# State carried between chunks of 128 tokens in place of scores across chunks, in a hybrid GLA and mLSTM block

## The chip, the cores and the metric

The kernel runs on one core of a Trainium2 chip. The metric is the device time of one execution in microseconds (us), and the figure given is the median over runs. The profiled execution is one more run, of which every instruction is recorded.

## The reference, cut to what matters

One layer of a block with two kinds of recurrent heads, four each: gated linear attention (GLA) and mLSTM. Both run over 512 latent tokens in both directions, starting from a state that 256 context tokens leave. Per head the key width is 128 and the value width 256. All is float32.

```python
# GLA, one direction:  S_t = diag(a_t) S_{t-1} + k_t v_t^T ;  o_t = S_t^T q_t
bcum = jnp.cumsum(ac, axis=2)                      # log decays within a chunk
k_to_end = kc * jnp.exp(b_end[:, :, None, :] - bcum)
s_new = jnp.exp(b_end)[..., None] * s + jnp.einsum('bhik,bhiv->bhkv', k_to_end, vc)
o = (jnp.einsum('bhji,bhiv->bhjv', scores, vc)     # scores within the chunk, with decays
     + jnp.einsum('bhjk,bhkv->bhjv', qc * jnp.exp(bcum), s))
# mLSTM, one direction: one forget gate and one input gate per token and head, running maximum m
c_new = carry_scale[..., None, None] * c + jnp.einsum('bhi,bhik,bhiv->bhkv', w, kc, vc)
n_new = carry_scale[..., None] * n + jnp.einsum('bhi,bhik->bhk', w, kc)
s = jnp.einsum('bhjk,bhik->bhji', qc, kc) * jnp.exp(d_log - m_q[..., None])   # masked
h = num / jnp.maximum(jnp.abs(den), jnp.exp(-m_q))[..., None]
```

The result does not depend on the chunk length: one may compute scores over any stretch of tokens and carry a state for the rest. Around this stand adaLN modulation, one input projection for all heads, a per-head norm with output gates, an output projection, and a gated feed-forward part with a 3x3 depthwise convolution.

## The kernel before, in words

The kernel runs in stages: modulation and the first projection (0 to 186 us), the heads (186 to 822), the output gates (to 965) and the output projection (to 1090), then the feed-forward part. Large products are done in three matmuls of float32r parts (`mm3`): each weight block is loaded as `raw`, ACT casts it to `hi`, DVE subtracts to get `lo` (`load_split`). The products inside a head are plain float32, which the trace shows as two PE instructions each.

In the head stage PE's order is written out by hand (`pinned`, so every matmul keeps program order). `weave` mixes two generators: the stages of head h, and the projection of head h+1 (`project_steps`, six pieces per weight block, 1.04 to 1.44 us by its own estimate). Each `yield x` in a head's code asks for x us of projection work at that place, so that PE has something to do while DVE and ACT prepare the next product. What is left of the projection runs after the head. For heads 0 and 1 `first_stages` is used (both were projected together), for the others `stages`.

A head's float32 products go to PSUM through `psb`. Its pool `psB` has two banks; the other six (`psA`) hold the six projection results that are being accumulated. A bank is handed on when its last reader is done.

A GLA head (`gla`) works on four blocks of 128 tokens. `bt[d]` holds the running sum of log decays within each block, per direction d; `b2[d]` continues it over blocks. Scores within a block come in seven levels (distances 1, 2, 4 to 64): at each level the decays relative to a border are formed (`level_decays`: two DVE subtractions, two ACT exponentials), multiplied by q and k (DVE), multiplied on PE (`sl`, four products) and put into `scd` where a mask says so (DVE `copy_predicated`). Two more levels, 128 and 256, cover scores across blocks, using `b2` and its values at block ends (`ends`), and are copied to `sc1` and `sc2` by ACT. After level 1 the state of the context `s0` is formed (`cst`), and `qi`, q with its decay since the start. The output `po` of each block is the sum of six products: `qi` with `s0` for both directions, the block's own scores with v, and the scores of three other blocks with their v. While levels 2 to 6 run, the preparation of the next head (`gla_prep`) advances one step after each of them through `next(after, None)`: two decay products `dec` (one per direction, 512 tokens), two `cdec` (context), then `csum`. Each of the first four is followed by `log_sigmoid`, three ACT operations and one DVE operation (`la`, `cla`), which reads the bank again at its end.

An mLSTM head (`mlstm`) forms for both directions the exponentials `ed` of the gates for all pairs of blocks on the causal side (ACT), zeroes half of the diagonal blocks (POOL `affine_select`), multiplies them by the scores `s` (PE, four products of 512 columns; DVE), and sums into `po` one product with the context state `c0` and one per block on the causal side, for each block and direction. The value tile has two more columns of ones, which give the denominator. `ml_gates`, after the last GLA head, prepares per-token columns `acol`, `thr`, and `wc` for the context.

During mLSTM heads and later, `fill()` inserts pieces of the modulation (`mod_chunk`: two DVE operations on 512 columns; `mod_sums`, `mod_end`: small PE products through `psb`).

Of the kernel before, what the change touches and what calls it, by code (L numbers as in the profile page):

```python
# [11 lines left out]
F32 = mybir.dt.float32  # L12
# [6 lines left out]
P = 128  # L19
# [51 lines left out]
def block_kernel(ctx: ExitStack, tc: tile.TileContext, a: dict, out: bass.AP):  # L71
# [411 lines left out]
    gccol = states.tile([P, 2, H], F32, name="gccol")  # L483
    wc = states.tile([P, 2, CJ, H], F32, name="wc")
# [168 lines left out]
    def gla_prep(h, out):  # L653
# [36 lines left out]
        yield  # L690

        b2 = [ytile(10 + d, f"b2{h}{d}") for d in range(2)]
        for d in range(2):
            order = list(range(TJ)) if d == 0 else list(range(TJ - 1, -1, -1))
            j = order[0]
            V.tensor_copy(b2[d][:, P * j : P * j + P], bt[d][:, P * j : P * j + P])
            for p, j in zip(order, order[1:]):
                e = P * p + P - 1 if d == 0 else P * p
# [3 lines left out]
        ends = wtile(f"ends{h}", "ends", 2, 2, 3)  # L702
        for d in range(2):
            src = b2[d][:, P - 1 : 3 * P : P] if d == 0 else b2[d][:, P : 3 * P + 1 : P]
            for i, sgn in enumerate((-DECAY, DECAY)):
                V.tensor_scalar(out=ends[:, i, d, :], in0=src, scalar1=sgn, scalar2=None, op0=ALU.mult)
        out.update(bt=bt, b2=b2, kd=kd, ends=ends)
# [28 lines left out]
    def gla(h, pair, qk, v, kn, vn, yT, prep, fill, after, pending):  # L736
        bt, b2, kd, ends = (prep[n] for n in ("bt", "b2", "kd", "ends"))

        sc = wtile(f"sc{h}", "sc", 2, TJ, P)
        scd, sc1 = sc[:, 0], sc[:, 1]  # L740
        sc2 = [ytile(12 + i, f"sc2{h}{i}", (P, 2, 2 * P)) for i in range(2)]
        s0 = wtile(f"s0{h}", "state", 2, DV + 2)
        ps = psb(f"sd{h}", (P, TJ, P))
# [5 lines left out]
        for lv, b in enumerate(LEVELS + [P, 2 * P]):  # L749
            if b < P:  # L750
                ex = prep["ex"][lv] if lv < 2 else level_decays(h, lv, bt)
            else:
                ex = wk2.tile([P, 2, T], F32, name=f"ex{h}_{lv}", tag="ex")
                for i in range(T // (2 * b)):
                    e = 2 * i if b == P else 1
                    for s in range(2):
                        for d in range(2):

                            at = 2 * b * i + (b if s == d else 0)
                            S.activation(ex[:, s, at : at + b], b2[d][:, at : at + b], AF.Exp,  # L760
                                         scale=-DECAY if s else DECAY, bias=ends[:, s, d, e : e + 1])
# [5 lines left out]
            if b <= P:  # L767
                ps = psb(f"sl{h}_{lv}", (P, TJ, P))
                for i in range(TJ):
                    j = i if b < P else i ^ 1  # L770
                    mm(ps[:, i, :], ex[:, 1, P * i : P * i + P], ex[:, 0, P * j : P * j + P], start=True, stop=True)
                if b < P:
                    V.copy_predicated(scd, msk[:, lv, :].unsqueeze(1).to_broadcast([P, TJ, P]), ps)
                else:
                    S.copy(sc1, ps)
            else:
                for half in range(2):
                    ps = psb(f"sl{h}_{lv}_{half}", (P, 2, 2 * P))
                    for ii in range(2):
                        i = 2 * half + ii  # L780
                        j0 = 2 * P * (1 - half)
                        mm(ps[:, ii, :], ex[:, 1, P * i : P * i + P], ex[:, 0, j0 : j0 + 2 * P],
                           start=True, stop=True)
                    S.copy(sc2[half], ps)
            if lv == 0:
                pending()
            yield fill
            if lv in (2, 3, 4, 5, 6, 8):
                next(after, None)
            if lv == 1:  # L790

                for j in range(CJ):
                    mul(kd[:, :, j], kd[:, :, j], kn[j].unsqueeze(1).to_broadcast([P, 2, DK]))
                ps = psb(f"cst{h}", (P, 2, DV))
                for d in range(2):
                    for j in range(CJ):
                        mm(ps[:, d, :], kd[:, d, j, :], vn[j][:, 0:DV], start=(j == 0), stop=(j == CJ - 1))
                S.copy(s0[:, :, 0:DV], ps)
                qi = wtile(f"qi{h}", "qi", 2, T)
                for d in range(2):  # L800
                    S.activation(qi[:, d, :], b2[d], AF.Exp, scale=DECAY)
                mul(qi, qi, qk[0].unsqueeze(1).to_broadcast([P, 2, T]))
                yield 1
        ssq = wtile(f"ssq{h}", "ssq", TJ)
        junk = wtile(f"junk{h}", "kn", DV)
        ob = wtile(f"ob{h}", "tmp", TJ, DV)
        for j in range(TJ):
            po = psb(f"po{h}_{j}", (P, DV))
            js = slice(P * j, P * j + P)
            j2 = P * (j % 2)  # L810
# [11 lines left out]
    def ml_gates():  # L822
# [36 lines left out]
        dg = wk.tile([36, H], F32, name="dg", tag="st1")  # L859
        for d in range(2):  # L860
# [10 lines left out]
            end = TC - 1 if d == 0 else T  # L871
            V.tensor_scalar(out=negg[rows[d], :], in0=gmx[rows[d], lat0[d] : lat0[d] + T], scalar1=-1.0,
                            scalar2=None, op0=ALU.mult)
            V.tensor_scalar(out=dg[rows[d], :], in0=e, scalar1=gmx[rows[d], end : end + 1], scalar2=None, op0=ALU.mult)
            pg = psb(f"pgc{d}", (P, H))
            mm(pg, cst[rows[d], C_ONE : C_ONE + 1].to_broadcast([H, P]), dg[rows[d], :], start=True, stop=True)
            V.tensor_copy(gccol[:, d, :], pg)
            yield 1.4
        for d in range(2):
            for j in range(CJ):  # L880
                sub(wc[:, d, j, :], acol[:, d, j, :], gccol[:, d, :])
        S.activation(wc, wc, AF.Exp)

    def mlstm(h, _, qk, v, kn, vn, yT):
# [12 lines left out]
        for d in range(2):  # L897
# [4 lines left out]
            S.activation(qs[:, d, :], pg, AF.Exp, bias=gccol[:, d, hh : hh + 1])  # L902
            mul(qs[:, d, :], qs[:, d, :], q)
            ed = wk2.tile([P, 10 * P], F32, name=f"ed{h}{d}", tag="ex")
            at = 0
            spans = []
            for i in range(TJ):
                j0, j1 = (P * i, T) if d == 0 else (0, P * i + P)
                e = ed[:, at : at + j1 - j0]
                spans.append((e, j0, j1))  # L910
                at += j1 - j0
                S.activation(e, pg[:, j0:j1], AF.Exp, bias=acol[:, d, CJ + i, hh : hh + 1])
                blk = e[:, P * i - j0 : P * i - j0 + P]
                s = 1 if d == 0 else -1
                G.affine_select(out=blk, in_=blk, compare_op=ALU.is_ge, fill=0.0, base=0,
                                pattern=[[s, P]], channel_multiplier=-s)
            pd.append(spans)
        yield 4.2
        c0 = wtile(f"c0{h}", "state", 2, DV + 2)
        for d in range(2):  # L920
# [3 lines left out]
            S.copy(c0[:, d, :], ps)  # L924
        yield 1.4
        for i in range(TJ):
            ps = psb(f"s{h}{i}")
            mm(ps, k[:, P * i : P * i + P], q, start=True, stop=True)
            for d in range(2):
                e, j0, j1 = pd[d][i]  # L930
                mul(e, e, ps[:, j0:j1])
            yield 1.4
# [3 lines left out]
        for j in range(TJ):  # L936
            for d in range(2):
                po = psb(f"po{h}_{j}{d}", (P, DV + 2))
                js = slice(P * j, P * j + P)
                mm(po, qs[:, d, js], c0[:, d, :], start=True, stop=False)  # L940
                rng = range(j + 1) if d == 0 else range(j, TJ)
                for i in rng:
                    e, j0, _ = pd[d][i]
                    mm(po, e[:, P * j - j0 : P * j - j0 + P], v[i], start=False, stop=(i == rng[-1]))
# [20 lines left out]
    def first_stages(tiles):  # L965
# [12 lines left out]
        end = yield from gla(1, *tiles, yT, preps[1], 2.2, gla_prep(2, preps[2]), end)  # L978
# [4 lines left out]
    def stages(h, tiles):  # L983
# [4 lines left out]
        elif h + 1 < H:  # L988
            end = yield from gla(h, *tiles, yT, preps[h], 4, gla_prep(h + 1, preps[h + 1]), lambda: None)
# [3 lines left out]
        else:  # L993
            end = yield from gla(h, *tiles, yT, preps[h], 2.6, iter(()), lambda: None)
# [448 lines left out]
```

## Time and profile before

| | us |
|---|---|
| median of 3 runs (2512.5 to 2513.84) | 2513.63 |
| profiled execution | 2511.87 |
| its span on the core | 2510.1 |
| PE busy in the span | 2469.3 |
| weight loads (PEld) busy | 2204.1 |
| DVE busy | 1815.0 |
| ACT busy | 1024.0 |
| head stage, 186 to 822 us: length / PE / DVE / ACT busy | 636.0 / 628.3 / 350.1 / 225.3 |

The span is the time between the first and the last instruction of the core; the profiled execution's own time is 1.8 us longer. A line of the timeline gives start, length, engine, line of the kernel, operation, output and inputs, how many instructions were merged, and in brackets how long the engine had been idle before and for whom it waited. Matmuls overlap, so the time that one takes from its engine is read from one start to the next. Names in lines leave out buffer numbers: `sl` is any level's score tile.

### The profile page before, as it was taken

How to read it: one execution, taken by the hardware profiler on the slowest of the kernel's cores; microseconds unless marked ns; L12 is line 12 of the kernel's file. 1: busy time of each engine (PE TensorE's matmuls, PEld its weight loads, DVE VectorE, ACT ScalarE, POOL GpSimd, SP SyncE). 2: the span in 40 equal slices, each digit the busy share in tenths (PEclk: the TensorE clock that was granted, in tenths of full speed). 3: DMA queues.
4: the chain of work that ended last, by engine and by line, in shares of the span. 5: the costliest groups of instructions: out<-in, count | busy, mean ns of one | idle time of the engine just before them, and what ended most of it. 6: DMA issues, size and time to landing. Idle time of an engine off the chain costs nothing.

```text
span 2510.1 us, 39398 instructions
## 1 busy us (share of the span) xinstructions
PE 2469.3 (98%) x15740; PEld 2204.1 (88%) x15740; DVE 1815.0 (72%) x2880; ACT 1024.0 (41%) x1517; POOL 182.5 (7%) x242
## 2 busy tenths in 40 slices
PE   6999999999999999999999999999999999999998
PEld 4887889888987888888989999999999999999997
DVE  6666754554445877858988787878787878787886
ACT  4224543332213233226454444444444444444445
POOL 0000000000000000000020101010101010101022
PEclk9999999999999999999999999999999999999999
DMA  9741011123334878842373737373636363646464
GB/s 385 271 172 42 26 43 51 51 76 125 110 117 155 286 274 304 299 158 99 108 176 101 168 104 166 107 168 104 167 104 166 107 162 108 161 113 160 113 186 135
DMA packets 121552, 372.20 MB, mean 148 GB/s; under 512 B 13908, under 2 KB 18328, under 8 KB 121368
## 3 DMA queue, kind: packets, MB, share of 16 engines
q1 hardware_dynamic: 94680, 318.29, 37.7%
q0 software_dynamic: 25600, 50.34, 11.4%
q8 instruction: 123, 2.02, 0.3%
q10 hardware_dynamic: 1088, 1.05, 0.1%
q14 instruction: 61, 0.50, 0.1%
HBM read 319.30 MB, written 50.33 MB: 147 GB/s over the span
## 4 chain that ended last, share of the span: by engine, by line
PE 85%; issue 9%; DVE 2%; DMA 2%; POOL 1%; ACT 1%; SPq 0%; DVEq 0%; POOLq 0%; ACTq 0%
PE a L98 19%; PE dn L98 17%; PE uv L98 15%; PE ug L98 14%; PE ga L98 7%; PE po L98 4%; PE wo L98 3%; PE sl L98 1%; PE ps_m L98 1%; DMA raw_m<-in_w_mod 1%; PE cst L98 1%; PE s L98 1%; DMA xl<-in_xT 0%; POOL x2d L1269 0%; DMA x2d<-st 0%
## 5 line engine op out<-in xcount | busy, mean ns | idle before, releaser
L98 PE MATMUL dn<-gh,lo_d 128*128 128x512 f32 x672 | 262.3, 390 | 0.3 <-DVE lo_d L93 0.3
L98 PE MATMUL dn<-gh,hi_d 128*128 128x512 f32 x672 | 261.6, 389 | 0.0
L98 PE MATMUL dn<-gl,hi_d 128*128 128x512 f32 x672 | 261.6, 389 | 0.0
L1215 DVE SCALAR_TENSOR_TENSOR cv<-pads,cwt,cv 128x512 f32<-128x512 f32 x344 | 239.5, 748 | 0.6
L1269 POOL DMA_DIRECT2D x2d<-st x160 | 140.1, 928 | 1142.7 <-ACT st L1268 1057.5
L313 DVE SCALAR_TENSOR_TENSOR sum_m<-raw_m,csil,sum_m 128x512 f32<-128x512 f32 x240 | 180.1, 750 | 9.0 <-DMA raw_m<-in_w_mod 3.1
L93 DVE TENSOR_TENSOR lo_buv<-sum_uv,hi_buv 128x1024 fp32r<-128x1024 f32 x80 | 98.0, 1224 | 103.6 <-ACT hi_buv L92 103.6
L98 PEld LDWEIGHTS dn<-gh,lo_d 128*128 128x128 f32 x672 | 126.1, 188 | 28.9 <-DVE lo_d L93 2.6
L98 PE MATMUL a<-hi_h,hTh 128*128 128x256 f32 x512 | 150.4, 294 | 0.5 <-ACT e L406 0.5
L98 PEld LDWEIGHTS dn<-gl,hi_d 128*128 128x128 f32 x672 | 126.2, 188 | 25.9
L98 PEld LDWEIGHTS dn<-gh,hi_d 128*128 128x128 f32 x672 | 126.2, 188 | 25.6
L98 PE MATMUL a<-hi_h,hTl 128*128 128x256 f32 x512 | 144.7, 283 | 0.0
L98 PE MATMUL a<-lo_h,hTh 128*128 128x256 f32 x512 | 144.7, 283 | 0.0
L92 ACT CAST hi_d<-raw_d 128x1024 fp32r<-128x1024 f32 x86 | 88.6, 1030 | 131.9 <-PE ug L98 70.6
L93 DVE TENSOR_TENSOR lo_d<-raw_d,hi_d 128x1024 fp32r<-128x1024 f32 x86 | 102.9, 1196 | 48.1 <-ACT hi_d L92 47.5
L98 PE MATMUL ug<-bth,hi_bug 128*128 128x256 f32 x480 | 136.7, 285 | 0.1
L98 PE MATMUL uv<-bth,lo_buv 128*128 128x256 f32 x480 | 135.9, 283 | 0.8 <-DVE lo_buv L93 0.8
L98 PE MATMUL uv<-bqh,lo_auv 128*128 128x256 f32 x480 | 135.9, 283 | 0.0
L98 PE MATMUL uv<-bth,hi_buv 128*128 128x256 f32 x480 | 135.9, 283 | 0.0
L98 PE MATMUL uv<-bql,hi_auv 128*128 128x256 f32 x480 | 135.8, 283 | 0.0
L98 PE MATMUL ug<-bqh,lo_aug 128*128 128x256 f32 x480 | 135.8, 283 | 0.0
L98 PE MATMUL uv<-btl,hi_buv 128*128 128x256 f32 x480 | 135.8, 283 | 0.0
(379 smaller groups left out, 7347.2 us busy)
## 6 DMA issues: line engine op xcount, KB each, us to landing
raw_m<-in_w_mod SPq DMA_DIRECT2D x192, 512.0 KB, 5.2
raw_d<-in_w_down SPq DMA_DIRECT2D x82, 512.0 KB, 3.4
raw_ug<-in_w_up SPq DMA_DIRECT2D x80, 512.0 KB, 3.5
x2d<-st POOLq DMA_DIRECT2D x160, 256.0 KB, 5.5
raw_uv<-in_w_up SPq DMA_DIRECT2D x80, 512.0 KB, 6.2
raw_h<-in_w_heads SPq DMA_DIRECT2D x64, 512.0 KB, 3.6
raw_ga<-in_w_gates SPq DMA_DIRECT2D x32, 512.0 KB, 4.5
raw_wo<-in_w_out SPq DMA_DIRECT2D x32, 512.0 KB, 4.8
```

What stands on the lines that cost most here:

```text
L92: cast[0] = S.copy(hi, x).ins
L93: return V.tensor_tensor(out=lo, in0=x, in1=hi.bitcast(F32), op=ALU.subtract).ins
L98: ins = PE.matmul(*args, **kw)
L313: V.scalar_tensor_tensor(out=parts[0], in0=x, scalar=ck, in1=parts[0], op0=ALU.mult, op1=ALU.add)
L1215: V.scalar_tensor_tensor(out=t3, in0=src, scalar=w, in1=t3, op0=ALU.mult, op1=ALU.add)
L1269: nc.gpsimd.dma_start(x2d[k], t, accum_op=ALU.add)
```

## The change

Both kinds of heads now compute scores only within a block of 128 tokens and carry a state from block to block, in both directions.

GLA: the levels 128 and 256, `b2`, `sc1` and `sc2` go. `ends` holds the decay of whole blocks and its exponential. After level 1, `kt` is formed: k with the decay up to its block's end, for three blocks in each direction (six ACT exponentials of 128 columns, two DVE multiplies of 384). After level 2, six PE transposes turn it into `ktt`, through two `psb` banks and two ACT copies. After levels 3, 4 and 5, one step of the state each: two products into one bank and two DVE operations (`st`). `po` is the sum of three products: `qi` with the state of either direction, and the block's own scores with v. The fill per level goes from 2.2 to 2.75, 4 to 5 and 2.6 to 3.25.

mLSTM: `gcol` holds the running maximum at every block border, and `wc` also the weights of keys up to their block's end and the factors of the state. k is transposed on PE (four transposes) and scaled into `ktt`; `s` is four products of 128 columns; six state products follow, two per stage, each in a bank of its own; `po` is the sum of two products. `ed` is formed for the four diagonal blocks only.

```diff
@@ gla_prep
-        b2 = [ytile(10 + d, f"b2{h}{d}") for d in range(2)]
-        for d in range(2):
...
-                V.tensor_scalar(out=b2[d][:, P * j : P * j + P], in0=bt[d][:, P * j : P * j + P],
-                                scalar1=b2[d][:, e : e + 1], scalar2=None, op0=ALU.add)
...
+        ends = wtile(f"ends{h}", "ends", 2, 2, TJ - 1)
         for d in range(2):
+            at = P * d + (P - 1) * (1 - d)
+            V.tensor_scalar(out=ends[:, 0, d, :], in0=bt[d][:, at : at + 2 * P + 1 : P], scalar1=DECAY, scalar2=None,
+                            op0=ALU.mult)
+        S.activation(ends[:, 1], ends[:, 0], AF.Exp)
@@ gla
-        for lv, b in enumerate(LEVELS + [P, 2 * P]):
+        for lv, b in enumerate(LEVELS):
...
-            if lv in (2, 3, 4, 5, 6, 8):
+            if lv in (2, 3, 4, 5, 6):
                 next(after, None)
...
-                    S.activation(qi[:, d, :], b2[d], AF.Exp, scale=DECAY)
+                    S.activation(qi[:, d, :], bt[d], AF.Exp, scale=DECAY)
                 mul(qi, qi, qk[0].unsqueeze(1).to_broadcast([P, 2, T]))
                 yield 1
+                kt = [ytile(10 + d, f"kt{h}{d}", (P, TJ - 1, P)) for d in range(2)]
+                for d in range(2):
+                    for i in range(TJ - 1):
+                        S.activation(kt[d][:, i, :], bt[d][:, P * (i + d) : P * (i + d) + P], AF.Exp, scale=-DECAY,
+                                     bias=ends[:, 0, d, i : i + 1])
+                    x = kt[d].rearrange("p a b -> p (a b)")
+                    mul(x, x, qk[1][:, P * d : P * d + 3 * P])
+            elif lv == 2:
+                ktt = [ytile(12 + d, f"ktt{h}{d}", (P, TJ - 1, P)) for d in range(2)]
+                for d in range(2):
+                    ps = psb(f"ktt{h}{d}", (P, TJ - 1, P))
+                    for i in range(TJ - 1):
+                        tr(ps[:, i, :], kt[d][:, i, :], ident)
+                    S.copy(ktt[d], ps)
+            elif lv > 2 and lv < 6:
+                n = lv - 3
+                if n:
+                    st.append(ytile(9 + n, f"st{h}{n}", (P, 2, DV)))
+                ps = psb(f"st{h}{n}", (P, 2, DV))
+                for d, i in ((0, n), (1, 2 - n)):
+                    mm(ps[:, d, :], ktt[d][:, i, :], v[i + d][:, 0:DV], start=True, stop=True)
+                for d, i in ((0, n), (1, 2 - n)):
+                    V.scalar_tensor_tensor(out=st[n + 1][:, d, :], in0=st[n][:, d, :], scalar=ends[:, 1, d, i : i + 1],
+                                           in1=ps[:, d, :], op0=ALU.mult, op1=ALU.add)
...
-            parts = [(qi[:, d, js], s0[:, d, 0:DV]) for d in range(2)]
-            parts += [(scd[:, j, :], v[j][:, 0:DV]), (sc1[:, j ^ 1, :], v[j ^ 1][:, 0:DV])]
-            far = 1 if j < 2 else 0
-            parts += [(sc2[far][:, i, j2 : j2 + P], v[2 * far + i][:, 0:DV]) for i in range(2)]
+            parts = [(qi[:, d, js], st[3 - j if d else j][:, d, :]) for d in range(2)]
+            parts.append((scd[:, j, :], v[j][:, 0:DV]))
@@ ml_gates
+            for n in range(TJ):
+                end = TC + P * n - 1 if d == 0 else T - P * n
+                V.tensor_scalar(out=dg[rows[d], n, :], in0=e, scalar1=gmx[rows[d], end : end + 1], scalar2=None,
+                                op0=ALU.mult)
...
+            sub(wc[:, d, CJ : CJ + 3, :], acol[:, d, CJ + d : CJ + d + 3, :], ends)
+            sub(wc[:, d, CJ + 3 :, :], g[:, 0:3, :], g[:, 1:TJ, :])
@@ mlstm
+            for i in range(TJ):
+                js = slice(P * i, P * i + P)
+                n = TJ - 1 - i if d else i
+                S.activation(e[:, i, :], pg[:, js], AF.Exp, bias=acol[:, d, CJ + i, hh : hh + 1])
+                S.activation(qs[:, d, js], pg[:, js], AF.Exp, bias=gcol[:, d, n, hh : hh + 1])
...
         yield 4.2
+        ps = psb(f"ktt{h}", (P, TJ, P))
+        for i in range(TJ):
+            tr(ps[:, i, :], k[:, P * i : P * i + P], ident)
+        ktt = [ytile(14, f"ktt{h}0", (P, TJ - 1, P)), wtile(f"ktt{h}1", "cla", TJ - 1, P)]
+        for d in range(2):
+            V.tensor_tensor(out=ktt[d], in0=ps[:, d : d + 3, :],
+                            in1=wc[:, d, CJ : CJ + 3, hh : hh + 1].to_broadcast([P, TJ - 1, P]), op=ALU.mult)
...
-        for i in range(TJ):
-            ps = psb(f"s{h}{i}")
-            mm(ps, k[:, P * i : P * i + P], q, start=True, stop=True)
+        ps = psb(f"s{h}", (P, TJ, P))
+        for i in range(TJ):
+            js = slice(P * i, P * i + P)
+            mm(ps[:, i, :], k[:, js], q[:, js], start=True, stop=True)
+        for d in range(2):
+            mul(pd[d][0], pd[d][0], ps)
+        yield 1.4
+        for n in range(TJ - 1):
+            for d, i in ((0, n), (1, 2 - n)):
+                ps = psb(f"st{h}{d}{n}", (P, DV + 2))
+                mm(ps, ktt[d][:, i, :], v[i + d], start=True, stop=True)
+                V.scalar_tensor_tensor(out=st[d][n + 1], in0=st[d][n], scalar=wc[:, d, CJ + 3 + n, hh : hh + 1],
+                                       in1=ps, op0=ALU.mult, op1=ALU.add)
             yield 1.4
...
-                mm(po, qs[:, d, js], c0[:, d, :], start=True, stop=False)
-                rng = range(j + 1) if d == 0 else range(j, TJ)
...
+                mm(po, qs[:, d, js], st[d][TJ - 1 - j if d else j], start=True, stop=False)
+                mm(po, pd[d][0][:, j, :], v[j], start=False, stop=True)
@@ first_stages, stages
-        for need in (0, 1.4, 0, 3, 1, 0):
+        for need in (0, 1.4, 0, 3, 1):
...
-        end = yield from gla(0, *tiles, yT, preps[0], 2.2, gla_prep(1, preps[1]), lambda: None)
+        end = yield from gla(0, *tiles, yT, preps[0], 2.75, gla_prep(1, preps[1]), lambda: None)
...
-            end = yield from gla(h, *tiles, yT, preps[h], 4, gla_prep(h + 1, preps[h + 1]), lambda: None)
+            end = yield from gla(h, *tiles, yT, preps[h], 5, gla_prep(h + 1, preps[h + 1]), lambda: None)
```

More of the change, by code (lines that the diff above doesn't have):

```diff
@@ L748, in gla @@
         yield fill
-        for lv, b in enumerate(LEVELS + [P, 2 * P]):
[L750 to L761, printed above, removed]
+        for lv, b in enumerate(LEVELS):
+            ex = prep["ex"][lv] if lv < 2 else level_decays(h, lv, bt)
             if pair:
@@ L766, in gla @@
                     mul(ex[:, i, :], ex[:, i, :], qk[i])
-            if b <= P:
-                ps = psb(f"sl{h}_{lv}", (P, TJ, P))
-                for i in range(TJ):
[L770 to L784, printed above, removed]
+            ps = psb(f"sl{h}_{lv}", (P, TJ, P))
+            for i in range(TJ):
+                js = slice(P * i, P * i + P)
+                mm(ps[:, i, :], ex[:, 1, js], ex[:, 0, js], start=True, stop=True)
+            V.copy_predicated(scd, msk[:, lv, :].unsqueeze(1).to_broadcast([P, TJ, P]), ps)
             if lv == 0:
@@ L858, in ml_gates @@
         yield 13
-        dg = wk.tile([36, H], F32, name="dg", tag="st1")
+        dg = wk.tile([36, TJ, H], F32, name="dg", tag="st1")
         for d in range(2):
@@ L977, in first_stages @@
                  [e[:, 0:DK] for e in c], [e[:, DK:] for e in c])
-        end = yield from gla(1, *tiles, yT, preps[1], 2.2, gla_prep(2, preps[2]), end)
+        end = yield from gla(1, *tiles, yT, preps[1], 2.75, gla_prep(2, preps[2]), end)
         yield 4
@@ L993, in stages @@
         else:
-            end = yield from gla(h, *tiles, yT, preps[h], 2.6, iter(()), lambda: None)
+            end = yield from gla(h, *tiles, yT, preps[h], 3.25, iter(()), lambda: None)
             yield 5
```

65 lines of the change are left out of this document (20 added, 45 removed).

## The prediction

> **What bounds the kernel now.** I read the page first, then the windows of the head stage, then the waits of TensorE (PE), and last the timeline of single heads.
>
> ```profile
> span 2510.1 us, 39398 instructions
> PE 2469.3 (98%) x15740; PEld 2204.1 (88%) x15740; DVE 1815.0 (72%) x2880; ACT 1024.0 (41%) x1517; POOL 182.5 (7%) x242
> PE 85%; issue 9%; DVE 2%; DMA 2%; POOL 1%; ACT 1%; SPq 0%; DVEq 0%; POOLq 0%; ACTq 0%
> ...
> 186.00:822.00 636.00, 628.30 (x3722) 547.58 (x3721) 350.10 (x657) 225.31 (x449) 17.57 (x36) 1.00 0.25 81
> 350.00:425.00 75.00, 75.00 (x449) 67.15 (x448) 40.96 (x66) 32.84 (x66) 0.73 (x1) 1.00 0.14 43
> 520.00:605.00 85.00, 85.00 (x487) 75.20 (x487) 39.17 (x84) 24.02 (x47) 4.07 (x12) 1.00 0.35 112
> ...
> PE sl L98 <- DVE ex L84: 3.2, 3, 1.7
> PE cdec L98 <- DVE la L635: 1.7, 2, 1.1
> PE sl L98 <- DVE la L635: 1.0, 2, 0.7
> ```
>
> PE is busy for 98% of the span and carries 85% of the chain. The change lies wholly in the head stage, 186 to 822 us (window rows: PE, PEld, DVE, ACT, POOL busy, granted clock, DMA share, GB/s). There PE is idle for 636.00 - 628.30 = 7.7 us in all; the third GLA head (350 to 425) and an mLSTM head (520 to 605) have no idle time at all, while DVE works half of it and DMA about a third or less. So in this stage a microsecond of matmul removed comes off the end one for one, and a new wait of PE goes onto it one for one: nothing later has slack to take it up.
>
> **What goes and what comes on PE.** PE's time per instruction is read from start to start, not from durations, since matmuls overlap.
>
> ```profile
> 359.14 1.16 PE L98 MATMUL sl<-ex 128*128 128x128 f32 x8
> 360.05 0.42 PE L98 MATMUL a<-hi_h,hch 128*128 128x384 f32 x1
> ...
> 392.91 1.03 PE L98 MATMUL po<-s,qi 128*128 128x256 f32 x4
> 393.77 1.89 PE L98 MATMUL po<-v,sc 128*128 128x256 f32 x8
> ...
> 542.02 0.60 PE L98 MATMUL po<-c,qs 128*128 128x258 f32 x2
> 542.46 1.03 PE L98 MATMUL po<-v,ed 128*128 128x258 f32 x4
> ...
> 529.12 1.02 PE L98 MATMUL s<-qk 128*128 128x512 f32 x2
> 561.75 1.04 PE L103 MATMUL yt<-cst,ob 128*128 128x128 f32 x8
> ...
> L98 PE MATMUL s<-qk 128*128 128x512 f32 x32 | 16.3, 591 | 0.0
> L103 PE MATMUL yt<-cst,ob 128*128 128x128 f32 x64 | 8.5, 273 | 0.4 <-DVE sc L773 0.4
> ```
>
> A float32 product is two instructions in the trace: four products of `sl` show as x8, and eight transposes `yt` as x8, so a transpose is one. The steps: 128 columns, (360.05 - 359.14) / 8 = 0.11 us; 256 columns, (393.77 - 392.91) / 4 = 0.215; 258 columns, (542.46 - 542.02) / 2 = 0.22; 512 columns, 1.02 - 0.591 = 0.43; a transpose, (1.04 - 0.273) / 7 = 0.11.
>
> A GLA head loses the level of 128 (8 instructions x 0.11 = 0.88), the level of 256 (8 x 0.215 = 1.72) and half of the six products of each of four `po` (24 x 0.215 = 5.16): 7.76 us. It gains six transposes (0.66) and six state products of 256 columns (12 x 0.215 = 2.58): 3.24. Net -4.52, four heads -18.1.
>
> An mLSTM head's `s` goes from 8 x 0.43 = 3.44 to 8 x 0.11 = 0.88, and its `po` from 28 products to 16 (24 x 0.22 = 5.28 less): 7.84 off. It gains four transposes (0.44) and six state products of 258 columns (12 x 0.22 = 2.64): 3.08. Net -4.76, four heads -19.0. Together **-37.1 us of PE work**. The estimated fill between stages stays the same in sum (ten times 4 becomes eight times 5; 22 and 26 likewise; the mLSTM yields also), so no projection work is pushed behind a head.
>
> [...] I keep the start-to-start steps, because overlap is already taken out of them and the stage shows almost no idle time.
>
> **What the other engines get.** In a GLA head DVE loses the eight small operations of `b2` and two full multiplies, and gains two multiplies of 384 columns and six state updates from PSUM: about even. ACT loses twelve exponentials and three score copies, and gains six exponentials and two copies. In mLSTM, POOL's eight selects become two larger ones. The window rows give the cover: DVE 40.96 of 75 us, ACT 32.84. I price this work at nothing. It matters only where it hands a PSUM bank back to PE.
>
> **New waits for a bank.** Six of the eight banks hold the projection being accumulated; everything else in a head shares the two of `psb`, and PE's order is written out. Today no stretch between two fills asks for more than two banks in levels 2 to 6 (a decay product, then `sl`). After the change, in heads 0 to 2, level 2 asks for four (`dec`, `ktt`, `ktt`, `sl`) and levels 3 to 5 for three (`dec` or `cdec`, `st`, `sl`), with no fill in between. This is what a bank costs:
>
> ```profile
> 358.09 1.12 PE L98 MATMUL dec<-glr,wlr 17*128 17x512 f32 x2
> 359.24 0.60 ACT L632 ACTIVATE lt<-dec 128x512 f32<-128x512 f32 x1 [2.14 <-PE dec L98]
> 361.56 0.69 DVE L635 SCALAR_TENSOR_TENSOR la<-dec,lt 128x512 f32<-128x512 f32 x1
> ...
> 239.12 1.12 PE L98 MATMUL dec<-glr,wlr 17*128 17x512 f32 x2
> 243.38 0.71 PE L98 MATMUL cdec<-wlr,glr 17*128 17x128 f32 x4
> 243.74 0.68 DVE L635 SCALAR_TENSOR_TENSOR la<-dec,lt 128x512 f32<-128x512 f32 x1
> 244.47 1.16 PE L98 MATMUL sl<-ex 128*128 128x128 f32 x8 [0.39 <-DVE la L635]
> 246.12 0.42 DVE L635 SCALAR_TENSOR_TENSOR cla<-cdec,ct 128x256 f32<-128x256 f32 x1
> ...
> 278.41 0.66 PE L103 MATMUL yt<-cst,ob 128*128 128x128 f32 x4 [0.38 <-DVE sc L773]
> ...
> L924 ACT COPY c<-cst x8: 375/375/376, 527.0 to 774.6; 128x258 f32<-128x258 f32 x8
> L784 ACT COPY sc<-sl x8: 565/587/597, 258.8 to 462.3; 128x512 f32<-128x512 f32 x8
> L953 DVE SCALAR_TENSOR_TENSOR ob<-po,dn,ob x16: 483/484/486, 541.7 to 807.1; 128x256 f32<-128x256 f32 x16
> ```
>
> The row at 278.41 is the pattern itself: a third user of the two banks (`sl`, `yt`, `yt`) waits for the first one's last reader. The row at 244.47 shows who gets which bank: `cdec` had started at 243.38, before the `dec` of 239.12 was read out (243.74 + 0.68 = 244.42), and `sl` then waited for that. So banks go to whoever comes first, in the order they come free. A `dec` holds its bank from 358.09 to 362.25, 4.2 us.
>
> Level 2, counted from `dec`'s start: the first three transposes begin at 1.05 (359.14 - 358.09) and end at 1.05 + 2 x 0.11 + 0.273 = 1.54. ACT is then in `dec`'s first operation until 1.75; a 384-column copy, between 0.375 and 0.587, say 0.48, ends at 2.3. The second three end at 2.8; ACT is in `dec`'s next operation until 2.9 and copies until 3.4, and `sl`, which could start at 1.05 + 0.66 = 1.71, starts at 3.45: a wait of 1.75. If ACT does all three operations of `dec` first, `sl` takes `dec`'s bank at 4.2, a wait of 2.5. I take 2.1. Levels 3 to 5: `st` runs from 1.05 and ends at 1.05 + 3 x 0.215 + 0.38 = 2.07; its two updates take 0.48 each, so `sl`, due at 1.91, starts at 3.05: 1.15. With one 0.7 us operation ahead on DVE half of the time it is 1.5, with a 1.2 us one 2.4; I take 1.5. A head: 2.1 + 3 x 1.5 = 6.6 (5.2 to 9.7); three heads **+19.8** (15.6 to 29.1). Head 3 prepares no next head; only its level 2 waits, for the first copy: +0.4 (to 1.0). Queued behind these waits is PE alone, with the projection's products; nobody but the head's own next level waits for those.
>
> mLSTM, where the two banks of `pg` are read by sixteen exponentials of 128 columns (today 2 + 8 larger ones):
>
> ```profile
> 246.52 2.44 ACT L760 ACTIVATE ex<-b,ends 128x128 f32<-128x128 f32 x8
> ...
> 521.09 0.69 ACT L902 ACTIVATE qs<-pg,gccol 128x512 f32<-128x512 f32 x1 [5.42 <-PE pg L98]
> 525.07 1.57 ACT L912 ACTIVATE ed<-pg,acol 128x256 f32<-128x256 f32 x3
> 525.96 1.90 PE L98 MATMUL cst<-vn,kt 128*128 128x258 f32 x8
> ```
>
> At 2.44 / 8 = 0.3 each they take 4.9 us, and a weight cast of about 1 us falls between as today, so the second bank comes free near 527.0 in place of 526.64; the transposes take the first at 525.96, and `cst`, due at 526.4, waits 0.6. The shorter `po` come round to their banks sooner, 0.2. I take 0.8 a head (0 to 2), **+3.2** (0 to 8). The same shorter `po` in GLA: 0.2 a head, +0.8 (0 to 2).
>
> Back comes part of today's idle time: with PE held up, the waits of `cdec` and `sl` for `la` (1.7 + 1.0) have nothing left to wait for, **-2.7** (0 to -7.2, nearly all there is).
>
> Sum: -37.1 + 19.8 + 0.4 + 3.2 + 0.8 - 2.7 = **-15.6**. The profiled execution took 2511.87, its span 2510.1 and 1.8 around it, so 2496.3; it lies 1.8 under the median of the runs (2513.63), so the forecast for the median is **2498 us**. All lower bounds together: -37.1 + 15.6 + 0.4 - 7.2 = -28.3, 2485; all upper ones: -37.1 + 29.1 + 1.0 + 8.0 + 2.0 = +3.0, 2517.
>
> **The rivals.** *No wait worth naming* (0.12): the whole 37.1 comes off, 2476.5. For it: PE is fully busy and 40% of DVE and over half of ACT are free. Against it: the row at 278.41, and that the added products stand between two fills.
>
> *Banks go in turn, and slower* (0.09): if the two banks alternated strictly, the third user at levels 2 to 5 would wait until the decay is read out, which is DVE work queued behind the two new updates (0.97). A `dec` was held 244.42 - 239.12 = 5.3 us, a `cdec` 246.54 - 243.38 = 3.2. Waits: 5.3 - 1.4 = 3.9 at level 2, 5.3 - 1.91 + 0.97 = 4.4 at level 3, 3.2 - 1.5 + 0.97 = 2.7 at levels 4 and 5: 13.7 a head, 41.1 for three, -37.1 + 41.1 + 4.4 = +8.4, 2522. It turns slower from (37.1 - 4.4) / 12 = 2.7 us per place. Against it: the order of 243.38 and 244.47.
>
> *The clock falls in the new gaps* (0.04):
>
> ```profile
> 19.15 2.07 PE L98 MATMUL ss_l<-sq_l,cst 128*128 128x512 f32 x2 [19.15 <-DVE sq_l L87]
> 21.16 3.21 PE L98 MATMUL ps_m<-raw_m,cact 128*32 128x256 f32 x32
> 25.40 1.93 PE L98 MATMUL ps_m<-raw_m,cact 128*32 128x256 f32 x32
> ```
>
> After 19 us of idle time two products took 2.07 us against 1.02 for the same shape at 529.12, and the next 32 took 3.21 against 1.93: 2.3 us lost per cold start. The longest wait in the heads is 1.7 us, and every window of them has a granted clock of 1.00. If the three waits at level 2 were long enough, +7, 2505. [...]
>
> *Nothing measurable* (0.07): the waits of the forecast near their upper ends cancel the gain, 2509 to 2517.
>
> **Chances and range.** The forecast has the remaining 0.68. A difference of 0.2%, 5 us, is about what a measurement of this kernel can tell from none. Faster: 0.68 + 0.12 + 0.04, less 0.02 of the forecast's upper end, 0.82; same 0.09; slower 0.09. The range runs from 2481, halfway to the first rival, to 2511, short of the second.
>
> **What would show it.** Right: in the waits of PE, `sl` waiting for DVE's `st` updates about nine times, 1 to 2.5 us each, and `ktt` or `sl` waiting for ACT's `ktt` copy about four times; the head stage some 16 us shorter, with idle time near 29 us. Wrong: that idle time still under 10 us (first rival), or `ktt` and `sl` waiting for `la` and `cla` (second), or 512-column products near 0.8 us behind a gap (third). The forecast is wrong as a whole if the windows show PE work in 186 to 822 shrinking by much other than 37 us.

## The result and the profile after

After the change the kernel takes 2502.02 us (median of 5 runs, 2500.13 to 2506.09), before it 2513.63: a ratio of 0.996 [0.9948, 0.9971], 11.6 us less. The forecast was 2498 with a range of 2481 to 2511 and "faster". The time came out near it, but not every term behind it did, and the largest that was missing from the sum belongs to a rival that had been given 0.04.

The head of the page of the changed kernel. The execution that it shows took 2506.09 us, the slowest of the five, 5.8 less than the profiled one of before.

```profile
span 2504.4 us, 39124 instructions
PE 2446.1 (98%) x15620; PEld 2183.4 (87%) x15620; DVE 1823.6 (73%) x2878; ACT 1008.1 (40%) x1517; POOL 176.1 (7%) x218
...
PE 83%; issue 10%; DVE 3%; DMA 2%; ACT 2%; POOL 1%; SPq 0%; DVEq 0%; POOLq 0%; ACTq 0%
```

PE is busy 23 us less and the span is only 6 us shorter; DVE and ACT have each taken a per cent of the chain that was PE's. Where that happens is read from windows cut at landmarks that both kernels have: ACT's read of a head's first queries (L621) and the first product of the stage behind the heads. The three rows are heads 0 to 2, head 3 with the gates, and the four mLSTM heads. The columns are the length, then busy time of PE, PEld, DVE, ACT and POOL with instructions, the granted clock, the DMA share and GB/s. First before, then after.

```profile
185.94:415.54 229.60, 224.04 (x1409) 194.80 (x1408) 142.20 (x248) 107.84 (x220) 0.73 (x1) 1.00 0.12 38
415.54:505.84 90.30, 88.65 (x545) 78.98 (x544) 52.29 (x71) 28.80 (x54) 1.47 (x2) 1.00 0.19 59
505.84:821.86 316.02, 315.54 (x1769) 273.73 (x1768) 155.54 (x341) 88.58 (x175) 15.38 (x33) 1.00 0.36 118
```

```profile
185.74:427.27 241.53, 222.00 (x1343) 188.65 (x1342) 140.25 (x224) 99.64 (x210) 0.73 (x1) 0.96 0.12 36
427.27:512.67 85.40, 84.37 (x523) 74.78 (x522) 53.45 (x77) 23.69 (x41) 1.47 (x2) 1.00 0.20 62
512.67:814.73 302.06, 297.96 (x1737) 263.81 (x1736) 164.21 (x357) 87.09 (x199) 8.59 (x9) 1.00 0.39 123
```

The mLSTM heads gained 14.0 us and head 3 gained 4.9. Heads 0 to 2, which had 13.6 us of PE work taken out (three times 4.52), became 11.9 us *longer*: PE's idle time there rose from 229.60 - 224.04 = 5.6 to 241.53 - 222.00 = 19.5, and the granted clock fell from 1.00 to 0.96.

The waits of PE in the head stage of the changed kernel (who waits, for whom; us in total, times, the longest):

```profile
PE sl L98 <- DVE cla L635: 5.1, 4, 1.7
PE sl L98 <- DVE st L791: 3.7, 2, 2.4
PE cst L98 <- DVE ktt L911: 3.4, 3, 1.1
PE sl L98 <- DVE sc L791: 3.0, 3, 1.1
PE sl L98 <- ACT ktt L782: 2.3, 4, 0.6
PE yt L103 <- DVE ob L644: 2.2, 2, 1.4
PE ktt L103 <- ACT ktt L782: 1.7, 3, 0.6
PE cdec L98 <- DVE la L635: 1.7, 2, 1.1
```

`sl` waits nine times for DVE (5.1 + 3.7 + 3.0 = 11.8 us), as often as forecast, though four of the nine end with `cla` and not with an update of the state. `sl` and `ktt` wait seven times for ACT's copies (4.0 us), where about four were forecast. The timeline of one head shows each (start, us, engine, line; in brackets the idle time before it and who ended it). First level 2, then 3, then 5 of head 0:

```profile
236.41 1.12 PE L98 MATMUL dec<-glr,wlr 17*128 17x512 f32 x2
237.47 0.55 PE L103 MATMUL ktt<-cst,kt 128*128 128x128 f32 x3
238.07 0.47 ACT L782 COPY ktt<-ktt 128x384 f32<-128x384 f32 x1
238.59 0.55 PE L103 MATMUL ktt<-cst,kt 128*128 128x128 f32 x3 [0.58 <-ACT ktt L782]
239.18 0.48 ACT L782 COPY ktt<-ktt 128x384 f32<-128x384 f32 x1
239.71 1.16 PE L98 MATMUL sl<-ex 128*128 128x128 f32 x8 [0.57 <-ACT ktt L782]
...
243.94 1.13 PE L98 MATMUL st<-v,ktt 128*128 128x256 f32 x4
245.22 0.87 DVE L791 SCALAR_TENSOR_TENSOR sc<-s,ends,st 128x256 f32<-128x256 f32 x2
246.13 1.16 PE L98 MATMUL sl<-ex 128*128 128x128 f32 x8 [1.07 <-DVE sc L791]
247.37 0.68 DVE L635 SCALAR_TENSOR_TENSOR la<-dec,lt 128x512 f32<-128x512 f32 x1
...
257.90 1.29 DVE L84 TENSOR_TENSOR ex<-ex,e 128x512 f32<-128x512 f32 x2 [0.76 <-ACT ex L717]
259.11 0.47 DVE L791 SCALAR_TENSOR_TENSOR st<-st,ends,st 128x256 f32<-128x256 f32 x1
259.59 0.42 DVE L635 SCALAR_TENSOR_TENSOR cla<-cdec,ct 128x256 f32<-128x256 f32 x1
259.93 0.47 DVE L791 SCALAR_TENSOR_TENSOR st<-st,ends,st 128x256 f32<-128x256 f32 x1
260.16 1.13 PE L98 MATMUL sl<-ex 128*128 128x128 f32 x8 [1.44 <-DVE cla L635]
```

At level 2 ACT copies the first three transposes at once, ahead of `dec`'s operations, and `sl` starts 239.71 - 236.41 = 3.30 after `dec` (forecast: 3.45). At level 3 both updates of the state have to be done before `sl` has a bank. The `dec` of that level is read out only by the `la` of 247.37, after `sl` has started, so the banks do not go strictly in turn, which speaks against the second rival. At level 5 other work of DVE comes first (`ex`, then `cla` between the two updates), and `sl` takes the bank of `cdec`, which `cla` had released, 0.4 us before the second update ends. In the mLSTM heads three of four show this pair:

```profile
534.50 1.01 DVE L911 TENSOR_TENSOR ktt<-ktt,wc 128x384 f32<-128x384 f32 x2
535.65 1.11 PE L98 MATMUL cst<-vn,kt 128*128 128x258 f32 x4 [1.14 <-DVE ktt L911]
```

And this is the clock. Two pairs of windows around waits of heads 0 to 2 (granted clock third from the end); the first stands behind `cdec`'s waits for `la`, the second behind the wait of level 5 in head 1:

```profile
209.80:213.20 3.40, 2.00 (x12) 1.69 (x13) 3.37 (x6) 2.92 (x9) 0.00 (x0) 1.00 0.00 0
213.20:216.60 3.40, 3.40 (x13) 3.40 (x12) 3.40 (x7) 1.90 (x6) 0.00 (x0) 0.50 0.02 5
316.00:321.00 5.00, 2.58 (x12) 2.16 (x11) 2.99 (x7) 2.77 (x7) 0.00 (x0) 0.80 0.34 93
321.00:326.00 5.00, 5.00 (x27) 4.27 (x26) 2.54 (x4) 2.47 (x5) 0.00 (x0) 0.85 0.05 17
```

In the first pair a stretch in which PE idles 1.4 of 3.4 us is followed by one at a granted clock of 0.50, PE busy throughout. The trace has five stretches at 0.50 in heads 0 to 2 (at 213, 295, 319, 340 and 384 us), each 3.41 us long. By estimate each loses half its length, 1.71: 8.5 us. Three of them (295, 319, 384) come behind the waits just shown, the one at 340 behind `yt` waiting for `ob`. The one at 213 comes behind a wait that the kernel before has too (`cdec` for `la`, 1.7 us in both). The profiled execution of before has no such stretch in these heads, but that is one execution: e2 below leaves them as before and lost the clock at the same place (0.50 from 214.05 to 217.46).

So heads 0 to 2 add up as -13.6 (work) + 14.0 (idle) + 8.5 (clock) = +8.9 of the +11.9. Idle time is counted from the end of the product ahead, and that end lies about 0.16 us beyond the product's step (0.273 against 0.11, 0.38 against 0.215), where without a wait the next one would already run. These heads have 20 waits of PE in place of 8 before, which makes another 12 x 0.16 = 2 us. The last 1 us is not placed.

### The profile page after: what moved, and what is told of

Its sections match the earlier page's. It is cut to its first block, busy times and chain, and to the rows that moved or that the text cites. A ratio compares the mean times of both kernels' runs of the same rounds, so it can differ in the third digit from the quotient of the medians.

```text
span 2504.4 us, 39124 instructions
## 1 busy us (share of the span) xinstructions
PE 2446.1 (98%) x15620; PEld 2183.4 (87%) x15620; DVE 1823.6 (73%) x2878; ACT 1008.1 (40%) x1517; POOL 176.1 (7%) x218
## 3 DMA queue, kind: packets, MB, share of 16 engines
q0 software_dynamic: 25600, 50.34, 11.3%
## 4 chain that ended last, share of the span: by engine, by line
PE 83%; issue 10%; DVE 3%; DMA 2%; ACT 2%; POOL 1%; SPq 0%; DVEq 0%; POOLq 0%; ACTq 0%
PE a L98 18%; PE dn L98 17%; PE uv L98 15%; PE ug L98 14%; PE ga L98 7%; PE wo L98 3%; PE po L98 2%; PE ps_m L98 1%; PE sl L98 1%; DMA raw_m<-in_w_mod 1%; PE st L98 1%; PE cst L98 0%; DMA xl<-in_xT 0%; DVE lo_h L93 0%; POOL x2d L1268 0%
## 5 line engine op out<-in xcount | busy, mean ns | idle before, releaser
L98 PE MATMUL ug<-bqh,hi_aug 128*128 128x256 f32 x480 | 135.8, 283 | 0.0
```

The source lines that it names most:

```text
L98: ins = PE.matmul(*args, **kw)
```

## The experiments

The theory was that the change removes the PE work forecast and puts waits for the two `psb` banks in its place, in heads 0 to 2 above all, and that the lost clock follows from those waits. The rivals were that the work removed is worth less than counted, that the loss sits in the mLSTM heads, and that DVE has too much to do between fills, whatever PE's order. The kernels e1 to e4 and e5 to e8 ran beside kernel before at 2513.72 and 2513.41 us.

**Each half alone.** The GLA half, with mLSTM and gates as before, and the mLSTM half, with GLA and its fill as before:

```diff
# e1: out of the changed kernel
-        ktt = [ytile(14, f"ktt{h}0", (P, TJ - 1, P)), wtile(f"ktt{h}1", "cla", TJ - 1, P)]
-                mm(po, qs[:, d, js], st[d][TJ - 1 - j if d else j], start=True, stop=False)
+                mm(po, qs[:, d, js], c0[:, d, :], start=True, stop=False)
...
# e2: out of the changed kernel
-        for lv, b in enumerate(LEVELS):
+        for lv, b in enumerate(LEVELS + [P, 2 * P]):
-            elif lv == 2:
-                ktt = [ytile(12 + d, f"ktt{h}{d}", (P, TJ - 1, P)) for d in range(2)]
...
```

> The GLA half of the change alone; the mLSTM heads and their gates are as before. Theory (new waits for the two shared PSUM banks eat the saved matmuls in heads 0 to 2, and the clock gate makes it worse): no gain or a small loss, 2511 to 2520 us, with about 20 us of PE idle time up to the third head and several stretches of half clock there. Rival A (the saved matmuls are smaller than worked out, waits do not matter): a gain of some 8 us, 2505, as half of the change. Rival B (the loss sits in the mLSTM heads): 2495, the full 18 us.

> The mLSTM half of the change alone; the GLA heads are as before. Theory: nearly the whole gain is here, -14 us, 2499 to 2500, and no half clock in the head stage. Rival A: -4, about 2509. Rival B: no gain, 2513.

e1 took 2520.03 us, ratio 1.0024 [1.0015, 1.0033]: **the GLA half alone makes the kernel 6.3 us slower**, at the upper end of what was expected. e2 took 2500.26, 0.9947 [0.9935, 0.996]: 13.5 us faster, more than both halves together (11.6). Windows of e1, heads 0 and 1 and the mLSTM heads, then of e2 at 214 us:

```profile
186.00:324.42 138.42, 125.23 (x770) 103.13 (x769) 90.15 (x141) 59.28 (x123) 0.00 (x0) 0.95 0.11 35
511.80:827.84 316.04, 315.56 (x1769) 273.90 (x1768) 155.52 (x341) 88.48 (x175) 15.41 (x33) 1.00 0.37 118
...
210.64:214.05 3.41, 2.28 (x14) 1.97 (x14) 3.41 (x8) 2.38 (x7) 0.00 (x0) 1.00 0.01 0
214.05:217.46 3.41, 3.41 (x15) 3.41 (x15) 3.41 (x13) 2.28 (x4) 0.00 (x0) 0.50 0.02 7
```

The loss stands where the changed kernel has it (13.2 us idle in two heads, clock 0.95), and the mLSTM heads are those of before. No half clock was expected in e2's head stage; it has one stretch, at 214 us, although its heads 0 to 2 are those of before. The halves add: the head stage ends at 827.84 in e1, 808.30 in e2 and 821.86 before, which gives 814.28 for both; the changed kernel ends it at 814.73.

**Another place for the same waits.** In e3 the next head's decay step comes behind the state step, not ahead of it. In e4 the fill of levels 2 to 5 is also cut in two, half ahead of the state step and half between it and the decay step, so that no stretch between two fills asks for more than two users of the banks.

```diff
# e3
             yield fill
-            if lv in (2, 3, 4, 5, 6):
-                next(after, None)
...
                                            in1=ps[:, d, :], op0=ALU.mult, op1=ALU.add)
+            if lv in (2, 3, 4, 5, 6):
+                next(after, None)
# e4, the same and
-            yield fill
+            yield fill / 2 if 2 <= lv <= 5 else fill
...
+            if 2 <= lv <= 5:
+                yield fill / 2
```

> The whole change, but in levels 2 to 6 of the GLA heads the step of the next head's preparation (dec, cdec, csum) is issued after the state step in place of ahead of it. No work, no fill and no bank is added or taken away; a decay product now runs while the state's bank is being read out. Theory (bank waits): the wait of sl at levels 3 to 5 falls by the length of the decay products, from about 1.1 to 0.3 us, that at level 2 to about 0.4; 10 to 13 us of waits go, and with them most of the half clock (another 5 to 8): 2482 to 2489. Rival C (heads 0 and 1 are slow because DVE has too much to do between fills, whatever PE's order): within 4 us of the changed kernel, 2498 to 2506.

> As the kernel with the state step first, and the fill of levels 2 to 5 is cut in two halves, one ahead of the state step and one between it and the decay product, so that no stretch between fills asks for more than two banks. Theory (bank waits): the waits for st, ktt and la at these levels go altogether, 2480 to 2486, a little under the kernel with the order alone. Rival C: 2498 to 2506. Rival D (half a fill of 1.1 to 1.4 us is too short for DVE, and sl waits for its ex instead): 2488 to 2495, with waits of sl for ex.

e3 took 2494.5, 0.9922 [0.9909, 0.9936]: better than the changed kernel by 7.5, but between what the theory (2482 to 2489) and the rival (2498 to 2506) expected. Its timeline at level 3 of head 0 shows why:

```profile
243.39 0.48 DVE L789 SCALAR_TENSOR_TENSOR sc<-s,ends,st 128x256 f32<-128x256 f32 x1 [0.46 <-PE st L98]
243.79 1.22 DVE L93 TENSOR_TENSOR lo_h<-raw_h,hi_h 128x1024 fp32r<-128x1024 f32 x1
244.92 0.47 DVE L789 SCALAR_TENSOR_TENSOR sc<-s,ends,st 128x256 f32<-128x256 f32 x1
245.45 1.16 PE L98 MATMUL sl<-ex 128*128 128x128 f32 x8 [1.05 <-DVE sc L789]
```

A split of the projection's input (1.22 us) got between the two updates on DVE. An earlier start of `st` did not help where its reader queued behind other work. e4 took 2481.88, 0.9873 [0.9859, 0.9886], 31.8 less than before. Its heads 0 to 2, and what is left of the waits:

```profile
185.79:404.05 218.26, 212.93 (x1343) 183.71 (x1342) 137.85 (x224) 99.38 (x210) 0.73 (x1) 0.99 0.13 40
...
PE cst L98 <- DVE ktt L913: 3.4, 3, 1.1
PE yt L103 <- DVE ob L644: 2.2, 2, 1.4
PE cdec L98 <- DVE la L635: 1.7, 2, 1.1
```

All sixteen waits of `sl` and `ktt` are gone, with the same number of instructions on PE in these heads (1343). The heads are 11.3 us shorter than before in place of 11.9 longer, idle time is back at 5.3, and one half-clock stretch, 1.7 by estimate, is left (granted clock 0.99 in the row), behind `yt` waiting for `ob`: without it -13.0, against the -13.6 of work removed.

**The fill.** In e5 the changed kernel has the old fills per level, 2.2, 4 and 2.6 in place of 2.75, 5 and 3.25. As the levels 128 and 256 are gone, their sum is then smaller than before too (eight times 4 in place of ten), and more of the projection runs behind the heads.

```diff
-... gla(0, *tiles, yT, preps[0], 2.75, gla_prep(1, preps[1]), lambda: None)
+... gla(0, *tiles, yT, preps[0], 2.2, gla_prep(1, preps[1]), lambda: None)
...
-... gla(h, *tiles, yT, preps[h], 5, gla_prep(h + 1, preps[h + 1]), lambda: None)
+... gla(h, *tiles, yT, preps[h], 4, gla_prep(h + 1, preps[h + 1]), lambda: None)
...
```

> The whole change with the fill per level as it was (2.2, 4 and 2.6), so less projection work between the levels and more of it behind the heads. Theory (bank waits, which stand between two fills and so do not depend on their size): within 4 us of the changed kernel, 2500 to 2506. Rival C (DVE short of time between fills): clearly slower, 2510 or more, with sl waiting for its ex in heads 0 and 1.

It took 2508.7, 0.9984 [0.9975, 0.9993], 6.7 more than the changed kernel, where the theory expected at most 4 and the rival 2510 or more. The rival's sign, `sl` waiting for its `ex` in heads 0 and 1, did not show. Two waits that grew or are new, and heads 0 to 2:

```profile
PE sl L98 <- DVE st L791: 6.4, 3, 2.4
...
PE pgc L98 <- DVE dg L861: 1.3, 1, 1.3
...
186.00:425.72 239.72, 219.61 (x1342) 186.87 (x1341) 139.38 (x224) 98.83 (x210) 0.73 (x1) 0.97 0.11 36
```

In the profiled runs these heads are no longer than in the changed kernel (241.53), and the whole runs differ by 2507.74 - 2506.09 = 1.7 us. Over all runs the mean granted clock is 0.9935 in e5 and 0.995 in the changed kernel; 0.0015 of 2500 us is some 3.7 us, an estimate, by which more than half of the 6.7 is lost clock. The fill is also the time in which DVE works off what was queued, and 0.55 to 1 us less per level would leave the updates further behind; the longer waits for `st` fit that, but its price was not measured apart from the clock's.

**The clock.** In e6 PE keeps the changed kernel's order, and products of 128 columns that nobody reads run where it waited: two ahead of the second `ktt` and of level 3's `sl`, four ahead of `sl` of levels 4 to 6. They leave the waits for the banks and take away the idle time in them; where they run longer than a wait, they add to the time.

```diff
+    def idle(n):
+        for _ in range(n):
+            mm(idle_at[0], ident, ident, start=False, stop=False, skip_group_check=True)
...
+            if h < 3 and 3 <= lv <= 6:
+                idle(2 if lv == 3 else 4)
             ps = psb(f"sl{h}_{lv}", (P, TJ, P))
...
+                    if d and h < 3:
+                        idle(2)
                     ps = psb(f"ktt{h}{d}", (P, TJ - 1, P))
```

> The whole change, with products that nobody reads put into the waits of heads 0 to 2: two of 128 columns ahead of the second ktt and of the level 3 sl, four ahead of the sl of levels 4 to 6, written to 128 spare columns of a projection bank. The waits stay, but PE is at work in them. Theory E (the clock falls because PE is idle in these waits): the stretches of half clock in heads 0 to 2 go, all but the one at 213 us, and with them 4 to 7 us: 2495 to 2498. Rival F (the clock falls for another reason, such as the kind of products there): clock as before and 2502 to 2507, as the products are a little longer than some waits.

Its median, 2501.43 (0.9948 [0.9935, 0.996]), is that of the changed kernel, lies between the two forecasts, and by itself decides nothing. But its five runs fall in two groups: 2497.66 and 2497.77 with a mean granted clock of 0.998, and 2501.43 to 2501.71 with 0.995 to 0.996. The profiled one is of the first, and shows the full clock in heads 0 to 2:

```profile
185.69:420.40 234.71, 225.23 (x1439) 194.22 (x1438) 139.99 (x224) 99.61 (x209) 0.73 (x1) 1.00 0.11 37
```

There they are 6.8 us shorter than in the changed kernel's profile. That supports the clock as a cost apart from the waits, but less than the 6.8 suggest: the products stand in the waits of levels 2 to 6, while the stretches at 213 and 340 us, which were lost behind other waits, are absent from this run too. At most the other three, 5.1 us, can be put down to the filled waits. What the three slower runs lost, and where, was not recorded.

**The mLSTM wait.** In e7 the mLSTM half alone (as in e2) forms `ktt` one fill later, behind the copies of `c0`, so that `cst` no longer stands behind DVE's two reads of it.

```diff
         yield 4.2
-        ps = psb(f"ktt{h}", (P, TJ, P))
...
         yield 1.4
+        ps = psb(f"ktt{h}", (P, TJ, P))
...
         ps = psb(f"s{h}", (P, TJ, P))
```

> The mLSTM half alone (GLA as before), with ktt formed one fill later, behind the context state and just ahead of s, so that cst does not wait for the bank that DVE reads ktt from. Theory: the wait of cst for ktt, 1.14 us in three heads and what its start hides, goes: 2495 to 2497, against 2500.3 for the half alone. Rival G (a wait of st for the bank of s comes in its place): 2499 to 2502.

It took 2493.84, 0.9925 [0.9912, 0.9937], 6.4 less than e2 and a little more than was expected. Its four mLSTM heads:

```profile
505.16:802.04 296.88, 296.68 (x1737) 264.15 (x1736) 163.89 (x357) 87.00 (x199) 8.20 (x9) 1.00 0.38 126
```

With 0.2 us idle and the full clock, this is the change's PE work by itself: 316.02 - 296.88 = 19.14 us less, where the steps had said 19.0.

**Together.** e8 is e4 with e7's order and a longer fill ahead of the end of head 1:

```diff
# e4, with ktt behind c0 as in e7, and
-        yield 4
+        yield 7
         end()
```

> The fill of levels 2 to 5 cut in two around the decay product, ktt of mLSTM formed one fill later, and 7 in place of 4 us of fill ahead of the end of head 1. If the waits add up as separate terms: 2481.9 less 4 for mLSTM and 2 for the end of head 1, 2475 to 2478, with under 6 us of PE idle time left in the head stage. If a new wait takes their place: 2480 to 2482.

It took 2478.18 us (2475.99 to 2481.35), 0.9858 [0.9843, 0.9873]: 35 us less than before, 24 less than the change as it was made. That is at the slow end of the forecast for waits that add up (2475 to 2478). The longer fill did nothing: `yt` still waits 2.2 for `ob` at the end of head 1, and in e4 and e8 the same 24 products of the projection stand between the last `po` and that `yt`, so there was none left to fill with. Its profiled run, the slowest of four, loses one stretch of clock at 213 us (granted clock 0.99 from 185.85 to 307.81), and a long one from 469 us, where the gates begin:

```profile
465.00:469.00 4.00, 3.66 (x21) 1.87 (x20) 1.66 (x3) 1.99 (x3) 0.00 (x0) 1.00 0.00 0
469.00:482.65 13.65, 13.65 (x46) 9.02 (x45) 6.00 (x9) 2.85 (x4) 0.00 (x0) 0.50 0.13 40
```

13.65 us at half clock behind a stretch in which PE idled only 0.34 us, but with the gates' small products (`pre`, `16*4` in the trace against `128*128` for the projection's). It costs 6.8 by estimate, half its length.

## Why the prediction was right, and where it was not

*PE work, -37.1: held.* e7 has the mLSTM part at -19.14 for -19.0, with nothing else in the way; e4's heads 0 to 2 come to -13.0 for -13.6. The measurement bears out the start-to-start steps, in this stage where PE has almost no idle time (0.2 us of 296.88 in e7's mLSTM heads).

*Bank waits in heads 0 to 3, +20.2: mechanism and places right, size a little high.* The forecast counted from start to start, so 0.16 per wait goes onto the idle time shown: 11.8 + 9 x 0.16 = 13.2 for the forecast 3 x 4.5 = 13.5 at levels 3 to 5, and 4.0 + 7 x 0.16 = 5.1 for 6.7 at level 2, where ACT copied before `dec`'s second operation; 18.3 in all. Which reader releases `sl` differs by level, as DVE's queue has it. e4 removes them by PE's order and the place of the fill, with the same products, so they are the banks' and not the arithmetic's. The +0.8 for GLA's shorter `po` did not show: no `po` waits in the changed kernel.

*A wait not forecast:* `yt` for `ob`, 2.2, counted from start to start 2.5.

*mLSTM wait, +3.2: too small.* The forecast put the delay at ACT's exponentials, 0.6 a head. It was DVE's two reads of `ktt` (1.01 us for the pair), which the prediction had counted among work that costs nothing, though it also hands a bank to `cst`: 1.14 in three heads, and 302.06 - 296.88 = 5.2 for all four.

*Relief, -2.7: larger, and from other rows.* `cdec` waiting for `la` stayed at 1.7: it stands in head 0's own preparation, ahead of any new wait. What vanished were `sl` waiting for `ex` (3.2) and for `la` (1.0) and `csum` for `cla` (0.5): 4.7 in six waits, 5.7 counted from start to start.

*Clock, 0: this is the step that failed.* The rival "the clock falls in the new gaps" was priced at three long waits and held for unlikely, since the longest wait of before was 1.7 us and every window of its heads had the full clock. The longest wait of the changed kernel is 2.4 us, and the clock fell five times all the same, 8.5 us in the profiled run by estimate: three times behind the forecast's waits, once behind `yt`, and once behind a wait that was there before. It came on top of the forecast's waits, not in their place, so the two were not alternatives. That every window of before shows the full clock was read off one execution, and e2 shows that the same heads can lose a stretch. In the 3.41 us ahead of each of the five stretches 0.7 to 2.4 us of idle time stand; how much it takes was not shown.

*Fill, 0: not contradicted, and not tested by itself.* The change keeps the fill's sum by larger pieces. e5, with the old pieces and a smaller sum, is 6.7 us slower, by the estimate above more than half of it through the clock; no run has the old pieces with the full sum.

In all, for the profiled run's head stage: -37.1 + 18.3 (banks) + 2.5 (`yt`) + 5.2 (mLSTM) - 5.7 (relief) = -16.8 without the clock, where the forecast had -15.6, and -8.3 with its 8.5. The end of the stage moved by 814.73 - 821.86 = -7.1; 1.2 is not placed. PE's idle time in the stage is 24.7, where near 29 was forecast.

That run is 4 us above its median. Its fellows of 2500.1 and 2501.5 have a mean clock of 0.996, it and that of 2505.1 have 0.994. The median's run has 0.995 against about 0.997 before, by estimate 0.002 of 2500 us, 5 us of lost clock, and the median lies 4 above the forecast. So the waits and the work came out near the forecast, in part by luck, as wrong sizes cancelled, and the clock is what the sum lacked.

## What to carry to other kernels

Where an engine hardly idles (PE 0.2 of 296.88 us in e7's mLSTM heads), work taken off it counted in full by start-to-start steps: 19.14 us for 19.0. But each product added needs an output bank, and the price of a bank is the queue of the engine that reads it (`sl` waited up to 2.4 us for DVE's updates of the state). Spread the users of scarce banks over the fills, so that a reader's queue is worked off before the next user comes: that was worth 20 us here, waits and clock together, more than the whole change. Price short waits twice, once as idle time and once as lost clock: in the changed kernel five stretches of 3.41 us at half clock stood behind waits, 8.5 us by estimate.

## What the runs showed of the hardware

In heads 0 to 2 of the changed kernel's profiled execution the granted clock was 0.50 in five stretches of 3.41 us, and 1.00 in the 3.41 us ahead of each. In those PE idled 1.39, 0.74, 2.42, 1.91 and 0.97 us. Idle time alone does not tell them from others: PE idled 1.29 us from 251.00 to 254.40 and 1.43 from 257.80 to 261.20, and in the 3.40 us that followed the clock was 1.00 both times. In e8, 0.34 us of it, together with the small `pre` products, stood ahead of 13.65 us at 0.50. Behind the heads, where no experiment was made, both kernels' profiles have the clock at 0.50 for 3.4 us, from 1138.23 us in the changed kernel and from 1143.40 in kernel before; the 3.4 us ahead have one-column products (`ps_rms`) and 0.2 us of idle time. What it takes for the clock to fall was not shown. Of the experiments only e6 filled waits with products that nobody reads, and its profiled run had a granted clock of 1.00 in heads 0 to 2.
